# One block of a token mixer: z, i and g projected token by token, head norms from summed squares, and five small steps of two heads on VectorE instead of GpSimd

## The chip, the cores and the metric

The kernel runs on one core of a Trainium2 chip. The metric is the time of one execution on the device, in microseconds (us). Five engines work side by side, each through its own instructions in a fixed order: TensorE (PE) multiplies matrices and transposes, VectorE (DVE) and ScalarE (ACT) do elementwise work, GpSimd (POOL) does small steps and issues some DMAs, SyncE (SP) issues the loads of the weights.

## The reference, cut to what matters

The input x has T = 256 tokens of D = 2048 numbers, all float32. One layer is computed:

```
n = rms_norm(x)
q,k,v,z,a,b | q',f,i,g = n @ W_in          # 8 heads of 128 in each group
# 8 GDN heads: q,k,v = silu(conv4(q,k,v)); q,k normalized to length 1;
#   chunked gated delta rule in chunks of 64 (needs the inverse of unit lower matrices)
#   o = head_rms_norm(o) * silu(z)
# 8 HGRN2 heads: forget = lb + (1-lb) sigmoid(f); key = (1-lb) sigmoid(-f)
#   o = recurrence(silu(q'), key, i, log forget), in chunks of 64
#   o = head_rms_norm(o) * silu(g)
h = x + concat(o) @ W_out
h = h + relu(rms_norm(h) @ W1)^2 @ W2
out = rms_norm(h)
```

The columns of n @ W_in for one head are 4 times 128: q, k, v, z for a GDN head, q', f, i, g for an HGRN2 head.

## The kernel before, in words

**Products in float32.** A weight tile of 1 MB (128 x 2048) is loaded by SyncE. `split` (L120, L121) makes two halves of each 1024 columns: hi, a rounded copy made on ScalarE, and lo, the rest, made on VectorE by a subtraction. A product is hi x hi + hi x lo + lo x hi. There are three buffers for tiles and three for pairs of halves, so a tile's successor is loaded and split as its matmuls end.

**The input projection** (`project`, L286 to L328) makes two groups of 128 features at a time, from two tiles. The activations xT stand with features on partitions; the weights are the stationary operand, and 512 columns of xT (its hi and lo halves, 256 tokens each) move: L314 (hi weights, 512 columns), then L315 (lo weights, 256 columns). A group is the sum of both halves of its PSUM bank: ScalarE copies the one half, VectorE adds the other (L324), and a product with the row scales rB follows (L328). Results have features on partitions and tokens along the row. Each head calls it twice; 16 heads make 64 tiles and 1024 such pairs.

**The GDN heads.** `gdn_project` calls `project` for q, k and for v, z. `gdn_mix` convolves, applies silu to all four groups, transposes v on PE, normalizes q and k and forms the small matrices of the delta rule (products pk, L402 and L403). GpSimd writes blocks of these to a scratch tile in DRAM (scr_a, L412). After head 7, `gdn_invert` (L445 to L470) reads them back (L449) and inverts 16 x 16 blocks on GpSimd by 15 pairs of steps (L459, L461). `gdn_solve` then joins the blocks (L477 to L524: products pQ, pP, pX on PE with steps on VectorE between them) and makes the outputs of two heads at a time.

**The HGRN2 heads.** `hgrn_project` projects q', f and i, g. `hgrn_mix` (from L573) transposes i (L577), computes the gates (L579 to L591), the logarithm and its running sum (L599 to L603), decays at several levels (L608 to L627), small products pd and pa (L638 to L653), joins them into A (L656 to L670) and makes the output poh (L672, L673). Five kinds of small steps in it run on GpSimd: L600, L603, L612, the memset L617, and the pair L663.

**The norm of a head** (`finish_heads`, L420 to L440). The output has features on partitions, so the mean of its squares is taken across partitions, by products with a matrix of ones (L432, L433) on the squares' hi and lo halves; logarithm and exponential give the scale, two products on VectorE apply it and the gate (L436, L437; the gate silu(z) or silu(g) waits in the ring SZ), and a split writes hi and lo into yT, the operand of the output projection. It is called for two GDN heads at once and for one HGRN2 head.

**The order.** The code walks over 16 heads: the projection of head n + 1 stands ahead of the mix of head n, the solver ahead of the mix of head 9 (HGRN2 head 1), the inversion behind the mix of head 7. The framework's scheduler then sets the order on each engine from a simulated timeline, under the dependences and the buffers; at run time each engine takes its instructions strictly in that order.

**PSUM.** It has eight banks of 512 columns. The mixers use two called mx and two called sv (psM); the input projection uses four called acc (psA, opened at the start). When the mixers are done, psB opens on the four banks of psM (L679). **The output projection** (L768 to L791; its matmul is L782, y as the stationary operand and 512 columns of weights moving) makes its first 1024 columns in psA and the others in psB; then the MLP (from L811) begins.

## Time and profile before

| | |
|---|---|
| median of 3 runs | 1231.27 us (1229.66 to 1232.65) |
| the profiled execution | 1230.59 us |
| its span, first to last instruction | 1228.9 us |
| its mean granted clock of TensorE | 0.993 |

| stage, us of the span | length | PE busy | DVE busy | ACT busy | POOL busy | granted clock |
|---|---|---|---|---|---|---|
| 0 to 260: GDN heads | 260 | 257.8 | 228.3 | 180.0 | 87.7 | 1.00 |
| 260 to 310: inversion ends, solver | 50 | 45.5 | 39.6 | 30.4 | 22.1 | 0.93 |
| 310 to 438: HGRN2 heads | 128 | 128.0 | 110.1 | 90.1 | 18.5 | 1.00 |
| 438 to 486: last two heads, output projection | 48 | 47.5 | 38.3 | 29.6 | 6.8 | 1.00 |
| 486 to 537: rest of the output projection | 51 | 49.4 | 35.8 | 28.1 | 0.0 | 0.97 |
| 537 to the end: MLP and last norm | 691.9 | 683.7 | 602.7 | 418.9 | 1.1 | 1.00 |

The second table is put together from windows of the trace. An engine's busy time counts its instructions that compute; the issue of a DMA, semaphores and branches are not counted. The granted clock is the share of full speed that the chip let TensorE run at in the window. A row of a timeline shows the start, the duration from the first instruction to the end of the last, the engine, the line, and the operation with what it writes and reads; "x4" behind it means four in a row.

### The profile page before, as it was taken

The numbers are of one execution on the slowest core, as the hardware profiler recorded it, in microseconds if no ns is written. First come the engines' busy times: TensorE is split into PE (matmuls) and PEld (weight loads), VectorE is DVE, ScalarE is ACT, GpSimd is POOL, SyncE is SP. The second block draws the span as 40 slices with busy tenths as digits, with TensorE's granted clock in tenths as the row PEclk, the third lists the DMA queues.
The fourth block names the chain that finished last, engine by engine and source line by source line (L and its number), as shares of the span: only waits on it lengthen the run. The fifth ranks groups of instructions, "written<-read, shape, count | busy, mean of one in ns | idle before, by whom it ended". The sixth has DMA issues, their size and how long they took to land.

```text
span 1228.9 us, 18515 instructions
## 1 busy us (share of the span) xinstructions
PE 1211.9 (99%) x7058; PEld 1018.8 (83%) x7058; DVE 1054.7 (86%) x1487; ACT 777.1 (63%) x1096; POOL 136.2 (11%) x185
## 2 busy tenths in 40 slices
PE   9999999998999999999999999999999999999997
PEld 7888888887888887888888888888888888888886
DVE  7889998878789986779889889889998888989877
ACT  7667677665677765655565656566666665656653
POOL 0243433262011121000000000000000000000000
PEclk9999999998999999999999999999999999999999
DMA  9545555543336445556455545653866556556461
GB/s 337 171 149 178 182 179 188 183 161 121 127 111 233 170 169 176 211 200 234 146 203 205 210 144 195 240 199 134 324 233 214 197 177 226 186 199 215 170 232 69
DMA packets 37145, 233.46 MB, mean 190 GB/s; under 512 B 4696, under 2 KB 5728, under 8 KB 10176
## 3 DMA queue, kind: packets, MB, share of 16 engines
q1 hardware_dynamic: 34848, 229.83, 53.0%
q0 software_dynamic: 1632, 1.72, 0.9%
q8 instruction: 55, 0.90, 0.3%
q10 hardware_dynamic: 576, 0.74, 0.2%
q14 instruction: 34, 0.28, 0.1%
HBM read 227.67 MB, written 4.60 MB: 189 GB/s over the span
## 4 chain that ended last, share of the span: by engine, by line
PE 93%; POOL 2%; DVE 2%; DMA 1%; issue 1%; ACT 0%; POOLq 0%; SPq 0%; DVEq 0%
PE acc L314 17%; PE acc L812 9%; PE acc L811 9%; PE acc L813 9%; PE acc L315 9%; PE accb L811 9%; PE accb L812 9%; PE accb L813 9%; PE accb L782 4%; PE acc L782 4%; POOL X L461 1%; PE acc L823 1%; PE accb L823 1%; PE pk L402 1%; DMA X<-scr_a 1%
## 5 line engine op out<-in xcount | busy, mean ns | idle before, releaser
L121 DVE TENSOR_TENSOR lo<-w,hi 128x1024 fp32r<-128x1024 f32 (+1 forms) x422 | 487.6, 1171 | 91.5 <-ACT hi L120 81.7
L120 ACT CAST hi<-w 128x1024 fp32r<-128x1024 f32 (+1 forms) x422 | 413.2, 993 | 210.1 <-PE acc L812 55.6
L314 PE MATMUL acc<-xT,hi 128*128 128x512 f32 x1024 | 358.7, 397 | 1.1 <-ACT hi L120 1.1
L315 PE MATMUL acc<-xT,lo 128*128 128x256 f32 x1024 | 280.9, 284 | 0.3 <-DVE lo L121 0.2
L314 PEld LDWEIGHTS acc<-xT,hi 128*128 128x128 f32 x1024 | 189.3, 188 | 39.9 <-ACT hi L120 1.7
L315 PEld LDWEIGHTS acc<-xT,lo 128*128 128x128 f32 x1024 | 193.1, 189 | 7.4 <-DVE lo L121 2.1
L120 ACT CAST hi<-TT 128x1024 fp32r<-128x1024 f32 x88 | 92.0, 1052 | 77.5 <-issue 21.7
L121 DVE TENSOR_TENSOR lo<-TT,hi 128x1024 fp32r<-128x1024 f32 x88 | 106.9, 1222 | 30.3 <-ACT hi L120 27.4
L811 PE MATMUL acc<-hi,sets 128*128 128x512 f32 x260 | 101.5, 392 | 0.0
L812 PE MATMUL acc<-hi,sets 128*128 128x512 f32 x260 | 101.3, 390 | 0.0
L813 PE MATMUL acc<-lo,sets 128*128 128x512 f32 x260 | 96.1, 391 | 0.0
L811 PE MATMUL accb<-hi,sets 128*128 128x512 f32 x224 | 88.1, 393 | 0.0
L812 PE MATMUL accb<-hi,sets 128*128 128x512 f32 x224 | 87.4, 390 | 0.0
L951 POOL TENSOR_TENSOR fin<-fin,cst 128x1 f32<-128x1 f32 x2 | 1.1, 564 | 743.9 <-DVE fin L950 743.9
L813 PE MATMUL accb<-lo,sets 128*128 128x512 f32 x224 | 78.8, 392 | 0.0
L812 PE MATMUL acc<-hi,gs 128*128 128x512 f32 (+1 forms) x200 | 77.1, 385 | 0.0
L811 PE MATMUL acc<-hi,gs 128*128 128x512 f32 (+1 forms) x200 | 76.8, 386 | 0.0
L813 PE MATMUL acc<-lo,gs 128*128 128x512 f32 (+1 forms) x200 | 75.7, 386 | 0.0
L812 PE MATMUL accb<-hi,gs 128*128 128x512 f32 x188 | 73.2, 390 | 0.0
L811 PE MATMUL accb<-hi,gs 128*128 128x512 f32 x188 | 72.8, 390 | 0.0
L813 PE MATMUL accb<-lo,gs 128*128 128x512 f32 x188 | 72.6, 390 | 0.0
L851 DVE TENSOR_TENSOR TT<-w 128x1024 f32<-128x1024 f32 x44 | 53.7, 1220 | 5.9 <-DMA w<-in_w_ff_dram 5.9
(336 smaller groups left out, 2029.9 us busy)
## 6 DMA issues: line engine op xcount, KB each, us to landing
w<-in_w_ff_dram SPq DMA_DIRECT2D x128, 1024.0 KB, 5.0
w<-in_w_in_dram SPq DMA_DIRECT2D x61, 1024.0 KB, 4.9
w<-in_w_out_dram SPq DMA_DIRECT2D x16, 1024.0 KB, 4.9
w<-in_w_in_dram SPq DMA_DIRECT2D x12, 256.0 KB, 5.4
big<-in_xt_dram SPq DMA_DIRECT2D x8, 256.0 KB, 5.5
h<-in_x_dram SPq DMA_DIRECT2D x2, 1024.0 KB, 5.9
scr_h<-h SPq DMA_DIRECT2D x4, 512.0 KB, 5.1
tail<-scr_h SPq DMA_DIRECT2D x2, 1024.0 KB, 6.4
```

What stands on the lines that cost most here:

```text
L120: ACT.copy(hi, w)
L121: eng.tensor_tensor(out=lo, in0=w, in1=hi.bitcast(F32), op=ALU.subtract)
L314: PE.matmul(accs[g], lhsT=hi[:, kk, g, :], rhs=xT[:, k, :], start=(k == 0), stop=False)
L315: PE.matmul(accs[g][:, T:], lhsT=lo[:, kk, g, :], rhs=xT[:, k, 0:T], start=False, stop=(k == KT - 1))
L402: PE.matmul(pk0, lhsT=R[:, 1, 0:P], rhs=qk.rearrange("p a t -> p (a t)"), start=True, stop=True)
L461: POOL.tensor_tensor(out=X[:, j + 1:, 0:ncol], in0=X[:, j + 1:, 0:ncol], in1=t3, op=ALU.subtract)
L782: PE.matmul(accs[2 * hf + c], lhsT=st, rhs=ww[:, c * 512:(c + 1) * 512], start=(k == 0 and a == 0 and ww is hi), stop=(k == 2 * NH - 1 and ...
L811: PE.matmul(dst, lhsT=ah, rhs=bh, start=start, stop=False)
L812: PE.matmul(dst, lhsT=al, rhs=bh, start=False, stop=False)
L813: PE.matmul(dst, lhsT=ah, rhs=bl, start=False, stop=stop)
L823: PE.transpose(pt[:, c * P:(c + 1) * P], src[:, c * P:(c + 1) * P], ident)
L851: DVE.tensor_tensor(out=TT[:, 0:1024].rearrange("p (a c) -> p a c", a=2), in0=view(w, 0, [[1536, 2], [1, 512]]), in1=view(w, 512, [[-512, ...
```

## The change

**Token by token.** z of the GDN heads, and i and g of the HGRN2 heads, are no longer made with features on partitions. `project_tokens` takes the activations as the stationary operand and moves 512 columns of weights: six matmuls for each 128 rows of the weights (L358), into two banks called tok that hold 128 tokens each by 512 columns. One tile of weights is a quarter of such a product. The 512 columns are z of four heads, or i and g of two heads, so results come out for four GDN heads or two HGRN2 heads at once, behind the last of their four tiles; each row is scaled while it is copied out (rcol, one number for each token, made in `row_scales`), and `silu` is applied to 512 columns at a time. q, k, v, q' and f stay as they were, v alone in a bank sv.

**The norm of a head.** The output is made with tokens on partitions (three products of 128 columns, L729 to L731 in `hgrn_mix`). Its squares are summed along the row by ScalarE's accumulated output; a scratch tile takes the squares themselves. One step on VectorE multiplies with scale and gate; PE transposes the result (L487); ScalarE and VectorE write hi and lo halves with the norm's weight. The products with ones and the transposes of i go.

**The five steps** of HGRN2 heads 0 and 1 run on VectorE, those of heads 2 to 7 on GpSimd as before (`eng`).

**PSUM.** The pool psA is opened behind the close of the mixers' pools; the input projection has a pool psP of its own, two banks acc and two banks tok, which closes with the mixers. On the host, the columns of W_in are put into tiles in the new order.

```
-    psA = ctx.enter_context(tc.tile_pool(name="psA", bufs=4, space=PSUM))
...
+    psP = mctx.enter_context(tc.tile_pool(name="psP", bufs=2, space=PSUM))
...
+    def acc_p(tag):
+        return psP.tile([P, 512], F32, tag=tag, name="acc")
...
+    def project_tokens(c):
+        if c == 0:
+            tok[0] = [acc_p("tok") for _ in range(2)]
+        accs = tok[0]
+        w, n = w_next()
+        for q, hi, lo in halves_of(w, n):
+            for kk in range(2):
+                k = c * 4 + q * 2 + kk
+                cs = slice(kk * 512, (kk + 1) * 512)
+                for hf in range(2):
+                    for a, ww in ((0, hi), (T, hi), (0, lo)):
+                        PE.matmul(accs[hf], lhsT=xT[:, k, a + hf * P:a + hf * P + P], rhs=ww[:, cs],
+                                  start=(k == 0 and a == 0 and ww is hi), stop=(k == KT - 1 and ww is lo))
...
+    def tokens_out(dst):
+        for hf in range(2):
+            ACT.activation(dst[:, hf, :], tok[0][hf], AF.Copy, scale=rcol[:, hf:hf + 1])
...
     def gdn_project(hd):
-        project(0, hd, 0, (pre[:, 0, 3:], pre[:, 1, 3:]))
-        project(0, hd, 1, (pre[:, 2, 3:], R[:, 3, :]))
+        project((pre[:, 0, 3:], pre[:, 1, 3:]), POOL, lambda: acc_p("acc"))
+        project((pre[:, 2, 3:],), POOL, lambda: sv("accv"))
+        project_tokens(hd % 4)
+        if hd % 4 == 3:
+            tokens_out(SZ[:, hd // 4])
+            for hf in range(2):
+                silu(SZ[:, hd // 4, hf])
...
     def finish_heads(h0, nh, po, sz, group, scale, bank):
-        ACT.activation(sq, po, AF.Square)
-        ACT.copy(shi, sq)
-        DVE.tensor_tensor(out=slo, in0=sq, in1=shi.bitcast(F32), op=ALU.subtract)
-        PE.matmul(pm, lhsT=ones_r, rhs=shi, start=True, stop=False)
-        PE.matmul(pm, lhsT=ones_r, rhs=slo, start=False, stop=True)
-        ACT.activation(sq, pm, AF.Ln, bias=eps, scale=scale / P)
-        ACT.activation(sq, sq, AF.Exp, scale=-0.5)
-        DVE.tensor_tensor(out=sq, in0=po, in1=sq, op=ALU.mult)
-        DVE.tensor_tensor(out=sq, in0=sq, in1=sz, op=ALU.mult)
+        at = [(hf, n, slice(n * P, (n + 1) * P)) for hf in range(2) for n in range(nh)]
+        for hf, n, c in at:
+            ACT.activation(sq, po[:, hf, c], AF.Square, accum_out=ss[:, hf, n:n + 1])
+        ACT.activation(ss, ss, AF.Ln, bias=eps, scale=scale / P)
+        ACT.activation(ss, ss, AF.Exp, scale=-0.5)
+        for hf, n, c in at:
+            DVE.scalar_tensor_tensor(out=sz[:, hf, c], in0=po[:, hf, c], scalar=ss[:, hf, n:n + 1],
+                                     in1=sz[:, hf, c], op0=ALU.mult, op1=ALU.mult)
+        for hf, n, c in at:
+            PE.transpose(pt[:, n * T + hf * P:n * T + hf * P + P], sz[:, hf, c], ident)
-        split(yv, None, hi, lo)
+        ACT.activation(hi, pt, AF.Copy, scale=gnw[:, group:group + 1])
+        DVE.scalar_tensor_tensor(out=lo, in0=pt, scalar=gnw[:, group:group + 1], in1=hi.bitcast(F32),
+                                 op0=ALU.mult, op1=ALU.subtract)
...
     def hgrn_mix(hd, R):
+        eng = DVE if hd < 2 else POOL
-        POOL.tensor_tensor(out=lf[:, 0, :], in0=lf[:, 0, :], in1=lf[:, 1, :], op=ALU.add)
+        eng.tensor_tensor(out=lf[:, 0, :], in0=lf[:, 0, :], in1=lf[:, 1, :], op=ALU.add)
...
     mctx.close()
...
+    psA = ctx.enter_context(tc.tile_pool(name="psA", bufs=4, space=PSUM))
     psB = ctx.enter_context(tc.tile_pool(name="psB", bufs=4, space=PSUM))
```

**Where instructions move: the inversion and the solver.** On GpSimd before, from the last write of GDN head 7's blocks (PA is the tile of its small matrices) to the first pair of the inversion (X and Xt its blocks; u, gx and E are tiles of HGRN2 head 0):

```order
L412 DMA scr_a<-PA_164 32x2x32 x4
L600 TENSOR_TENSOR u<-u 128x256
L603 TENSOR_SCALAR gx<-gx 128x256
L449 DMA X<-scr_a 64x16x16 x2
L612 TENSOR_TENSOR E<-gx 128x256
L453 AFFINE_SELECT X<-X 128x256
L455 MEMSET X 128x16
L459 TENSOR_TENSOR Xt<-X 128x15
L461 TENSOR_TENSOR X<-X,Xt 128x15
```

The same place after the change:

```order
L463 DMA scr_a<-PA_164 32x2x32 x4
L501 DMA X<-scr_a 64x16x16 x2
L505 AFFINE_SELECT X<-X 128x256
L507 MEMSET X 128x16
L511 TENSOR_TENSOR Xt<-X 128x15
L513 TENSOR_TENSOR X<-X,Xt 128x15
```

The three steps of head 0 (L600, L603, L612) have left GpSimd's queue; the load of the blocks now follows the writes directly.

On PE before, from the solver's second product (L490) to its third (L513), with the small products of an HGRN2 head between them (pd on E and gx):

```order
L490 MATMUL pQ<-Pm,Yd 32x16 x64
L638 MATMUL pd<-E 32x32 x32
L641 MATMUL pd<-gx 32x64
L513 MATMUL pP<-Xn,big 32x32 x20
L513 MATMUL pP<-Xn,PA_164 32x32 x12
```

After the change, the last rows ahead of the third product, now L565 (L358 is the token product; L331 and L332 are the feature pairs of the next head):

```order
L358 MATMUL acc<-hi,xT 128x512 x2
L358 MATMUL acc<-lo,xT 128x512
L358 MATMUL acc<-hi,xT 128x512 x2
L358 MATMUL acc<-lo,xT 128x512
L331 MATMUL acc<-xT,hi 128x512
L332 MATMUL acc<-xT,lo 128x256
L331 MATMUL acc<-xT,hi 128x512
L332 MATMUL acc<-xT,lo 128x256
L331 MATMUL acc<-xT,hi 128x512
L332 MATMUL acc<-xT,lo 128x256
L565 MATMUL pP<-Xn,big 32x32 x20
L565 MATMUL pP<-Xn,PA_164 32x32 x12
```

The two solver products stand further apart: between them lie 13 matmuls of L358, 6 of L331 and L332 and the three of an HGRN2 head's output, where 33 small products of a head lay before.

**Where instructions move: the last heads.** On PE before, at the small products of HGRN2 head 7 (pd, pa), with the output projection around them:

```order
L782 MATMUL acc<-hi,yTa 128x512 x8
L782 MATMUL acc<-lo,yTa 128x512
L638 MATMUL pd<-E 32x32 x32
L641 MATMUL pd<-gx 32x64 x8
L647 MATMUL pa<-E 32x32 x4
L651 MATMUL pa<-E 64x64 x2
L653 MATMUL pa<-L 128x128
L782 MATMUL acc<-lo,yTa 128x512 x3
L782 MATMUL acc<-hi,yTb 128x512 x4
```

After the change, from the last transposes of head 6 to the first matmuls of the output projection, now L847:

```order
L487 MATMUL pt<-cst,ig 128x128 x2
L695 MATMUL pd<-E 32x32 x32
L698 MATMUL pd<-gx 32x64 x8
L704 MATMUL pa<-E 32x32 x4
L708 MATMUL pa<-E 64x64 x2
L710 MATMUL pa<-L 128x128
L729 MATMUL poh<-ig,A 128x128
L730 MATMUL poh<-ig,A 128x128
L731 MATMUL poh<-ig,A 128x128
L487 MATMUL pt<-cst,ig 128x128 x2
L847 MATMUL acc<-hi,yTa 128x512 x4
L847 MATMUL acc<-lo,yTa 128x512 x2
```

All of head 7, to its transposes (L487), stands ahead of the first output-projection matmul; before, these matmuls stood around and between its products.

On VectorE before, at the same place, from head 7's level products (E) to the sum of its rows (rd), with head 6's norm (fsq) and the splits of weights (L121) between them:

```order
L623 TENSOR_TENSOR E<-E,gx 128x256 x5
L624 TENSOR_TENSOR E<-E,gx 128x512
L121 TENSOR_TENSOR lo<-w,hi 128x1024
L436 TENSOR_TENSOR fsq<-poh,fsq 128x256
L627 TENSOR_TENSOR L<-E,ec 128x256
L121 TENSOR_TENSOR lo<-w,hi 128x1024
L437 TENSOR_TENSOR fsq<-fsq,SZ 128x256
L121 TENSOR_TENSOR lo<-w,hi 128x1024
L121 TENSOR_TENSOR yTb<-fsq,yTb 128x256
L656 TENSOR_TENSOR pd<-pd,cst_a 128x384
L660 TENSOR_REDUCE rd<-pd 128x64
```

After the change:

```order
L665 TENSOR_TENSOR E<-gx 128x256 x5
L483 SCALAR_TENSOR_TENSOR ig<-poh,ss,ig 128x128 x2
L682 TENSOR_TENSOR gx<-gx,u 128x256
L680 TENSOR_TENSOR E<-E,gx 128x256 x5
L681 TENSOR_TENSOR E<-E,gx 128x512
L492 SCALAR_TENSOR_TENSOR yTb<-pt,gnw,yTb 128x256
L684 TENSOR_TENSOR L<-E,ec 128x256
L713 TENSOR_TENSOR pd<-pd,cst_a 128x384
L717 TENSOR_REDUCE rd<-pd 128x64
L483 SCALAR_TENSOR_TENSOR ig<-poh,ss,ig 128x128 x2
L492 SCALAR_TENSOR_TENSOR yTb<-pt,gnw,yTb 128x256
L121 TENSOR_TENSOR lo<-w,hi 128x1024 x13
```

The splits of weights no longer stand between the steps of head 7; they come in a row behind its last step (L492).

More of the change, by code (lines that the diff above doesn't have):

```diff
@@ new lines, in w_next @@
+    def w_next():
+        n = tiles[0]
+        tiles[0] += 1
+        if n < 2:
+            return w_first[n], n
+        w = wtile()
+        if n == 2:
+            for c in range(4):
+                SP.dma_start(w[:, c * 512:(c + 1) * 512], w_in[n][:, c * 512:(c + 1) * 512])
+        else:
+            SP.dma_start(w, w_in[n])
+        if n == 3:
+            SP.dma_start(cst, consts[:, 0:NKEEP])
+            SP.dma_start(cst_a, consts[:, NKEEP:])
+            SP.dma_start(wab, w_ab)
+        return w, n
@@ L316, in project @@
                                   start=False, stop=(k == KT - 1))
-        if second:
-            row_scales()
-            for lot, dst in held_back:
-                POOL.tensor_tensor(out=dst, in0=lot, in1=rB, op=ALU.mult)
-        for g in range(2):
+        for g in range(ng):
             lot = mp.tile([P, T], F32, tag="lot", name="lot", bufs=2)
             ACT.copy(lot, accs[g][:, T:])
-            DVE.tensor_tensor(out=lot, in0=accs[g][:, 0:T], in1=lot, op=ALU.add)
-            if first:
-                held_back.append((lot, dsts[g]))
-            else:
-                (POOL if base == 0 else DVE).tensor_tensor(out=dsts[g], in0=lot, in1=rB, op=ALU.mult)
@@ new lines, in gdn_solve @@
+            finish_heads(2 * pair, 2, po, SZ[:, pair // 2, :, pair % 2 * T:pair % 2 * T + T], 0, 1.0 / P, sv)
+    ig = [None]
+    def hgrn_project(hd):
+        R = mp.tile([P, 3, T], F32, tag="R", name="R", bufs=RB)
+        project((R[:, 0, :], R[:, 1, :]), DVE, lambda: acc_p("acc"))
+        for c in range(2):
+            project_tokens(hd % 2 * 2 + c)
+        if hd % 2 == 1:
+            ig[0] = mp.tile([P, 2, 512], F32, tag="ig", name="ig", bufs=2)
+            tokens_out(ig[0])
+            silu(ig[0][:, :, T:])
@@ L571, in hgrn_project @@
         return R
     def hgrn_mix(hd, R):
-        pv = mx("pvh")
-        for hf in range(2):
-            PE.transpose(pv[:, hf * P:(hf + 1) * P], R[:, 3, hf * P:(hf + 1) * P], ident)
-        vv = mp.tile([P, 2, P], F32, tag="vv", name="vv")
-        ACT.copy(vv.rearrange("p a e -> p (a e)"), pv[:, 0:T])
-        u = mp.tile([P, 4, T], F32, tag="u", name="u", bufs=UB)
-        sigmoid_parts(u[:, 0:3, :], R[:, 0:3, :], 3 * T)
-        DVE.scalar_tensor_tensor(out=u[:, 3, :], in0=R[:, 1, :], scalar=0.0, in1=u[:, 1, :], op0=ALU.max, op1=ALU.add)
@@ L691, in hybrid_block, with acc_a @@
     mctx.close()
+    psA = ctx.enter_context(tc.tile_pool(name="psA", bufs=4, space=PSUM))
     psB = ctx.enter_context(tc.tile_pool(name="psB", bufs=4, space=PSUM))
+    def acc_a():
+        return psA.tile([P, 512], F32, tag="acc", name="acc")
     def acc_b():
```

187 lines of the change are left out of this document (106 added, 81 removed).

## The prediction

> **What bounds the kernel now.** I read the busy line of the page first, then the waits of TensorE (PE), then the windows of the stages in which PE loses time. Times are those of the one profiled execution: a span of 1228.9 us, 1230.59 us with what lies around it, against a median of 1231.27 us of the runs shown; the sum below is made against 1230.6.
>
> ```profile
> PE 1211.9 (99%) x7058; PEld 1018.8 (83%) x7058; DVE 1054.7 (86%) x1487; ACT 777.1 (63%) x1096; POOL 136.2 (11%) x185
> PE accb L782 <- DVE fsq L436: 2.0, 1, 2.0
> PE pd L638 <- issue: 1.9, 1, 1.9
> PE poh L672 <- POOL Xt L459: 1.1, 1, 1.1
> PE pP L513 <- DVE Xn L492: 0.9, 1, 0.9
> PE pQ L484 <- DVE Xn L477: 0.2, 1, 0.2
> PE acc L315 <- DVE lo L121: 0.2, 1, 0.2
> 294.60:301.30 6.70, 5.61 (x106) 4.92 (x106) 6.55 (x15) 3.84 (x7) 0.10 (x1) 0.50 0.48 159
> 489.10:492.40 3.30, 3.30 (x9) 2.58 (x8) 2.37 (x3) 2.83 (x3) 0.00 (x0) 0.50 0.66 278
> ```
>
> PE is the bound: it is busy for all but 17 us. A change is therefore worth what it takes out of PE's own stream, or what it adds or closes in PE's idle time. From 260 us to 310 us, where GpSimd (POOL) inverts blocks and the solver starts, PE waits 1.9 + 1.1 + 0.9 + 0.2 + 0.2 = 4.3 us; at 485 us, where the mixers end, 2.0 us. The two windows (us, then busy time of PE, weight loads, VectorE, ScalarE and GpSimd, then the granted clock) show what follows each: 6.7 us and 3.3 us at a clock of 0.50, which lose half of their length, 3.35 us and 1.65 us. So the solver's place loses 4.3 + 3.35 = 7.7 us, and the end of the mixers 2.0 + 1.65 = 3.7 us.
>
> **PE's own work.**
>
> ```profile
> 134.12 0.40 PE L314 MATMUL acc<-xT,hi 128*128 128x512 f32 x1
> 134.35 0.28 PE L315 MATMUL acc<-xT,lo 128*128 128x256 f32 x1
> 134.47 0.39 PE L314 MATMUL acc<-xT,hi 128*128 128x512 f32 x1
> 448.82 8.42 PE acc L782 x37
> 469.83 0.38 PE L577 MATMUL pvh<-cst,R 128*128 128x128 f32 x2
> 469.96 0.71 PE L782 MATMUL acc<-lo,yTa 128*128 128x512 f32 x2
> 463.21 0.28 PE L432 MATMUL pm<-shi,ones_r 128*128 128x256 f32 x1
> 463.33 0.40 PE L782 MATMUL acc<-hi,yTa 128*128 128x512 f32 x1
> 457.08 0.59 PE L672 MATMUL poh<-A,vv 128*128 128x256 f32 x2
> 457.65 0.95 PE L782 MATMUL acc<-hi,yTa 128*128 128x512 f32 x3
> ```
>
> Matmuls overlap, so I count from start to start. A projection pair (512 columns, then 256) takes 134.47 - 134.12 = 0.35 us. The new token product has the form of the output projection, weights moving in 512 columns, and 37 of those took 8.42 us, 0.2276 us each. Three eighths of the 1024 pairs move: 384 x 0.35 = 134.4 us become 576 x 0.2276 = 131.1 us, **-3.3 us**; were they to run at the 0.23 us of the pair's long half, it would be 132.5 us and -1.9. The two transposes of a head's values cost 0.13 us and go 8 times, -1.0. The two ones-products of the normalization cost 0.12 us each at one head and, by the long half of the pair, 0.23 us at two: 8 x 0.24 + 4 x 0.46 = -3.8. Thirty-two transposes come in their place at 0.065, +2.1. The three products of 128 columns that give a head's output take the place of two that took 0.57 us together; with the same number of columns I put them at no change. Sum **-6.0 us** (bounds -4 and -7).
>
> **The five GpSimd steps, and the solver.**
>
> ```profile
> 240.35 2.13 POOL L412 DMA_DIRECT2D scr_a<-PA  x4 [17.08 <-DVE PA L406]
> 248.35 1.71 POOL L449 DMA_DIRECT2D X<-scr_a  x2
> 267.94 0.76 POOL L663 TENSOR_TENSOR A<-rd,cst_a 128x128 f32<-128x128 f32 x2
> 284.50 0.97 DVE L477 TENSOR_SCALAR Xn<-Xq,cst_a 128x256 f32<-128x256 f32 x2
> ```
>
> Before, the load of the blocks is issued at 248.35 because two steps of head 0 stand ahead of it on GpSimd's queue; the writes that it needs were issued by 242.5. A DMA of this tile lands in 3 us or so, so it could leave near 245.5. That and the pair of 0.76 us inside the inversion shorten the way from 240.35 to 284.50 (44.2 us) by about 3.7 us. But PE also arrives sooner: between the last GDN head's k products and the solver's first product the old order has 235 projection matmuls (117.5 pairs, 41.1 us), the new one 64 pairs and 66 long ones (22.4 + 15.0 = 37.4 us). The two shifts cancel, so the solver's first wait stays small; I allow 1 us. The waits for A at 268 us and on VectorE behind the first solver steps lose their cause: A no longer stands behind the inversion, and the solver's steps lie further apart in PE's new order. VectorE takes over 5 steps a head of some 0.3 to 0.4 us, under 4 us in all; it is idle beside PE for far more than that. I take **-6.7 us** of the 7.7; bounds 0 (the waits come back at other steps, and the clock falls again) and -9 (the bubbles between steps go too).
>
> **The end of the mixers.**
>
> ```profile
> 438.40:485.40 47.00, 42.87 (x180) 33.17 (x180) 1.00 0.53 180
> 446.92 0.73 PE L638 MATMUL pd<-E 128*32 128x32 f32 x62
> 448.57 1.18 PE L782 MATMUL acc<-hi,yTa 128*128 128x512 f32 x4
> 457.55 0.62 ACT L599 ACTIVATE u<-u 128x512 f32<-128x512 f32 x1
> 458.25 1.25 POOL L600 TENSOR_TENSOR u<-u 128x256 f32<-128x256 f32 x1 [5.08 <-ACT u L599]
> 459.71 0.68 DVE L602 TENSOR_TENSOR_SCAN gx<-cst_a,u 128x256 f32<-128x256 f32 x1
> 465.02 1.21 DVE L121 TENSOR_TENSOR lo<-w,hi 128x1024 fp32r<-128x1024 f32 x1
> 466.15 1.76 DVE L623 TENSOR_TENSOR E<-E,gx 128x256 f32<-128x256 f32 x5
> 467.83 0.69 DVE L624 TENSOR_TENSOR E<-E,gx 128x512 f32<-128x512 f32 x1
> 473.74 1.05 ACT L120 CAST hi<-w 128x1024 fp32r<-128x1024 f32 x1 [0.98 <-ACT yTb L120]
> 474.85 0.57 DVE L656 TENSOR_TENSOR pd<-pd,cst_a 128x384 f32<-128x384 f32 x1 [0.79 <-PE pd L641]
> 475.45 0.56 DVE L660 TENSOR_REDUCE rd<-pd 128x64 f32<-128x384 f32 x1
> 478.18 0.41 ACT L670 COPY A<-pa 32x64 f32<-32x64 f32 x2
> 482.79 0.39 ACT L426 ACTIVATE fsq<-poh 128x256 f32<-128x256 f32 x1 [0.28 <-PE poh L673]
> 1215.27 0.18 ACT L938 ACTIVATION_READ_ACCUMULATOR sqf<-tail 128x1 f32 x1
> 488.44 0.43 DVE L121 TENSOR_TENSOR yTb<-fsq,yTb 128x256 fp32r<-128x256 f32 x1 [0.47 <-ACT yTb L120]
> ```
>
> The first row is the window in which heads 6 and 7 of HGRN2 are mixed, counting L782 alone: 180 output-projection matmuls (41 us of stream) fill PE. They could, because their four banks (psA) stood beside the mixers' four. In the changed kernel psA is opened after the mixers' pools are closed, and PE's order has not one output-projection matmul until the last head's transposes. PE runs in order, so after the last input-projection matmul (call it P) it has nothing but the rest of two heads, and waits through a chain.
>
> I add that chain up by the new order. **(a)** Head 7's steps stand behind 1.05 us of cast and 1.21 of split for the next weights (their buffer comes free at P), a copy of new token sums (512 columns on ScalarE, 0.62), head 6's 0.57 and 0.56, and four steps of 256 columns at 0.3 to 0.4 (1.4); then its Ln, 0.62: 6.0 us. **(b)** GpSimd's add, 1.25. **(c)** From the scan to the end of L624, 459.71 to 468.52, is 8.8 us, less the split that lies between (465.02 to 466.15, 1.1): 7.7; head 6's two gating products stand inside it, an estimate of 0.6 from 0.43 for 256 columns. **(d)** Two more steps at 0.4: 0.8. **(e)** From L656 to the end of L670, 474.85 to 478.59, is 3.7 us with a pair of GpSimd products at 1.83; that pair took 0.76 at 267.94, when VectorE was idle, as it will be here: 2.7. **(f)** The output products at half clock 1.1, two squares with their accumulator reads (0.39 and 0.18 at most each) 1.0, two tiny steps 0.4, two gating products 0.6, two transposes 0.5, the two halves of the result 0.4 and 0.43: 4.4. Together 6.0 + 1.25 + 8.3 + 0.8 + 2.7 + 4.4 = **23.5 us** from P to the first output-projection matmul.
>
> Of these PE works 4.3 us on what it had to do anyway (a head's small products took 448.57 - 446.92 = 1.65 us, the output products 0.57 and the transposes 0.13; two heads, less what is done before P). The other 19.2 us are idle. The clock will be at half when the projection starts: by the two windows above, 1.65 to 3.35 us lost, I take 2.5. The 3.7 us lost there before go. **19.2 + 2.5 - 3.7 = +18.0 us**; bounds +13 (the chain is 5 us shorter) and +22 (every step of (a) and (b) waits for the one before it, and a product of GpSimd costs 1.8).
>
> The Trainium skill, "TensorE: Matmul & The Clock Gate", Part 1 (the HAM clock gate), says that the clock halves after about 3.4 us of idleness and comes back after about 3.4 us of work; by that the restart would cost half of 3.4, 1.7 us, and the sum would be 0.8 us less. The trace agrees with the way back at 489 us (3.3 us at 0.50) but not at 294 us (6.7 us), and there a wait of 2.0 us was enough to bring the clock down.
>
> The MLP is unchanged and begins when the output projection has ended, so all of this moves the end. **Sum: -6.0 - 6.7 + 18.0 = +5.3 us; 1230.6 + 5.3 = 1235.9, and I forecast 1236 us.**
>
> **Rivals.**
> - **The last head runs ahead (faster).** ScalarE and VectorE lose more work than they get: 24 additions of two halves (0.4 us), 16 gates and the wide normalization go. If head 7's Ln is done at P instead of P + 6, and (c) and (e) run without gaps, the projection starts near P + 14, 9.5 us sooner: 1226.5 us. It decides from P + 18 on downward (even) and P + 15.5 (faster by over 0.2%). Against it: in the new order head 7's sigmoid stands on ScalarE behind a cast that waits for the next-to-last weight tile's matmuls, so it can't start before about P - 5, however idle the engines are.
> - **The solver's wait comes back.** VectorE has the two heads' extra steps in just the stretch in which it bound (its windows there are full), PE waits again behind the solver, and the clock falls: the 6.7 us are not gained, 1242.6 us. For it: the two waits on VectorE at 292 to 297 us. Against it: the wider spacing in PE's new order.
> - **Even.** The exposed chain is 4 to 6 us shorter and the rest as computed: 1230 to 1233 us.
>
> **How the numbers follow.** Forecast 0.50 (its own range 1233.8 to 1240), solver's wait back 0.18 (to 1245 with a longer chain), even 0.19, last head ahead 0.13. A measurement of this kernel can tell about 0.2% (2.5 us) from no change, so slower 0.68, within 0.19, faster 0.13. The range leaves out 0.1 on each side: 1228 to 1244.
>
> **What would show it.** Right: in the changed profile PE has one idle stretch of some 19 us shortly after the last token product, with rows at clock 0.50 behind it; no output-projection matmul lies before the last transposes; the waits on GpSimd's inversion are gone; the last token product ends some 12 us earlier than the old 438 us. Wrong: PE's idle time at the end of the mixers is under 14 us, or the solver's stretch still shows a window at 0.50, or a token product takes over 0.235 us from start to start.

## The result, and the profile after

The changed kernel takes 1252.51 us (median of 4 runs, 1252.03 to 1253.72) against 1231.59 us: 1.0173 times as long, with a 95% interval of 1.0155 to 1.0191. That is 20.9 us more; 4.4 more had been forecast (1236), with a range that ended at 1244. The profiled execution has a span of 1250.2 us, 21.3 us over that of before.

The busy line of the page and the largest waits of TensorE (PE) in the two stages that the prediction named (us in total, times, longest):

```profile
PE 1221.6 (98%) x6894; PEld 1017.3 (81%) x6894; DVE 1035.3 (83%) x1455; ACT 777.0 (62%) x1150; POOL 113.4 (9%) x165
PE pt L487 <- DVE ig L483: 5.0, 2, 3.0
PE poh L729 <- POOL u L657: 4.4, 1, 4.4
PE pQ L536 <- DVE Xn L529: 2.4, 1, 2.4
PE pd L695 <- DVE E L680: 1.4, 1, 1.4
PE pp L584 <- ACT XP L578: 1.4, 1, 1.4
PE poh L729 <- POOL A L720: 1.2, 1, 1.2
PE acc L847 <- DVE yTb L492: 1.1, 1, 1.1
PE pP L565 <- DVE Xn L544: 0.7, 1, 0.7
```

PE has 164 matmuls fewer and is busy 9.7 us longer. Longer busy time with less work means time at a lower clock, so the windows are read next (us, then busy time of PE, weight loads, VectorE, ScalarE and GpSimd, then the granted clock; the last two numbers are what the DMA engines did):

```profile
294.70:302.00 7.30, 4.92 (x148) 4.21 (x148) 5.15 (x12) 2.20 (x4) 0.00 (x0) 0.77 0.07 18
321.80:324.00 2.20, 0.32 (x13) 0.08 (x2) 2.20 (x3) 2.15 (x4) 0.00 (x0) 0.63 0.23 30
324.00:339.60 15.60, 15.60 (x115) 13.44 (x116) 10.06 (x21) 4.27 (x13) 3.32 (x5) 0.50 0.17 65
444.40:467.20 22.80, 9.57 (x175) 7.41 (x160) 13.29 (x31) 11.32 (x33) 4.89 (x7) 0.59 0.13 48
467.20:472.40 5.20, 5.20 (x12) 4.13 (x13) 0.00 (x0) 0.54 (x1) 0.00 (x0) 0.50 0.00 0
```

The last two rows are the end of the mixers: 13.2 us without work, and nearly all of the 14.8 us of work in them at half clock. The third row is the surprise. In the solver's stage TensorE works without a break for 15.6 us, and all of it at a clock of 0.50.

To compare stages I use one measure, the **loss**: from windows of one microsecond each, PE's idle time, plus the part of its busy time that the clock withheld. Before, the solver's stage (180 to 360 us) lost 7.3 us and the end of the mixers 3.8 us. After, they lost 14.9 and 20.0 us. In the solver's stage most of this is the clock: idle time went from 4.5 to 5.4 us, what the clock withheld from 2.8 to 9.5. At the very start 0.4 us less is lost. So 21.3 = 7.6 (solver) + 16.2 (end) - 0.4 + the rest, and the rest, PE's own work, is -2.1 us. The MLP (from the start of its first matmul to that of its last) takes 682.9 us in both.

### The profile page after: what moved, and what is told of

Its sections match the earlier page's. It is cut to its first block, busy times and chain, and to the rows that moved or that the text cites. A ratio compares the mean times of both kernels' runs of the same rounds, so it can differ in the third digit from the quotient of the medians.

```text
span 1250.2 us, 18173 instructions
## 1 busy us (share of the span) xinstructions
PE 1221.6 (98%) x6894; PEld 1017.3 (81%) x6894; DVE 1035.3 (83%) x1455; ACT 777.0 (62%) x1150; POOL 113.4 (9%) x165
## 4 chain that ended last, share of the span: by engine, by line
PE 91%; POOL 2%; DVE 2%; DMA 2%; issue 1%; ACT 1%; SPq 0%; POOLq 0%; DVEq 0%; ACTq 0%
PE acc L877 9%; PE acc L878 9%; PE acc L876 9%; PE acc L358 9%; PE accb L877 8%; PE accb L876 8%; PE accb L878 8%; PE acc L331 8%; PE acc L332 4%; PE acc L847 4%; PE accb L847 3%; PE accv L331 2%; PE accv L332 1%; POOL X L513 1%; POOL Xt L511 1%
## 5 line engine op out<-in xcount | busy, mean ns | idle before, releaser
L121 DVE TENSOR_TENSOR lo<-w,hi 128x1024 fp32r<-128x1024 f32 (+1 forms) x422 | 485.7, 1167 | 123.4 <-ACT hi L120 112.3
L331 PE MATMUL acc<-xT,hi 128*128 128x512 f32 x512 | 181.2, 400 | 0.7 <-ACT hi L120 0.7
L332 PE MATMUL acc<-xT,lo 128*128 128x256 f32 x512 | 140.9, 287 | 0.0
L120 ACT CAST hi<-TT 128x1024 fp32r<-128x1024 f32 x88 | 92.0, 1052 | 77.5 <-issue 21.7
L121 DVE TENSOR_TENSOR lo<-TT,hi 128x1024 fp32r<-128x1024 f32 x88 | 106.8, 1221 | 30.4 <-ACT hi L120 28.1
L358 PE MATMUL acc<-hi,xT 128*128 128x512 f32 x384 | 117.6, 395 | 0.0
L331 PEld LDWEIGHTS acc<-xT,hi 128*128 128x128 f32 x512 | 95.4, 190 | 20.7 <-ACT hi L120 1.2
L332 PEld LDWEIGHTS acc<-xT,lo 128*128 128x128 f32 x512 | 97.2, 191 | 5.2 <-DVE lo L121 1.9
L358 PEld LDWEIGHTS acc<-hi,xT 128*128 128x128 f32 x384 | 71.5, 189 | 14.9
L358 PE MATMUL acc<-lo,xT 128*128 128x512 f32 x192 | 73.5, 401 | 0.0
```

The source lines that it names most:

```text
L120: ACT.copy(hi, w)
L121: eng.tensor_tensor(out=lo, in0=w, in1=hi.bitcast(F32), op=ALU.subtract)
L331: PE.matmul(accs[g], lhsT=hi[:, kk, g, :], rhs=xT[:, k, :], start=(k == 0), stop=False)
L332: PE.matmul(accs[g][:, T:], lhsT=lo[:, kk, g, :], rhs=xT[:, k, 0:T], start=False, stop=(k == KT - 1))
L358: PE.matmul(accs[hf], lhsT=xT[:, k, a + hf * P:a + hf * P + P], rhs=ww[:, cs], start=(k == 0 and a == 0 and ww is hi), stop=(k == KT - 1 a ...
```

## The experiments

Times are medians; the kernel before had medians of 1230.7 to 1231.1 us beside them. In the notes, "stage" is the solver's stage, 180 to 360 us.

**The five steps.** Three runs change only which engine takes them.

```
         eng = DVE if hd < 2 else POOL      # the change
-> e1:   eng = POOL
-> e2:   eng = DVE
-> e3:   the kernel before, with eng = DVE if hd < 2 else POOL in hgrn_mix
```

> The changed kernel with the five small steps on GpSimd for all eight HGRN2 heads, so that part of the change is undone. Its solver's stage lost about 15 us (waits and half clock) where 1 us was forecast. Theory A: the five steps of two heads are not what crowds VectorE (they are under 4 us in all); without them the load for the inversion stands behind GpSimd steps again, the solver's first product is reached 2 to 4 us later, and the time is 1253 to 1257 us. Rival B: the extra steps on VectorE are what holds the solver up; then the loss falls back to the 8 us of before and the time is 1244 to 1247 us.

Measured: 1248.78 us (1248.01 to 1253.59), 3.7 us under the changed kernel. Neither range is hit. The profiled execution is one of the longer ones (span 1251.9 us), so its stage, which lost 17.8 us, doesn't stand for the median. The steps on VectorE cost up to 3.7 us, about half of the 7.6 us by which the stage's loss grew; two of the five executions (1253.5 and 1253.6 us) gain nothing, so even this is not firm.

> The changed kernel with the five small steps on VectorE for all eight HGRN2 heads. In the changed kernel's trace VectorE stands still 1.6 and 0.8 us at 306 to 309 us, because steps of HGRN2 head 2 wait for GpSimd (L657, L660), and the solver's L544 stands behind them, its product done since 306.4 and the step begun only at 311.7; at the end of the mixers TensorE waits 4.4 and 1.2 us for GpSimd steps. Theory A (a queue behind GpSimd): 4 to 5 us go from the end and 3 to 8 us from the solver's stage: 1240 to 1246 us. Rival B (VectorE is simply full): the end gains 4 us, the solver's stage loses as much or more: 1249 to 1256 us.

Measured: 1248.12 us (1246.52 to 1252.09), 4.4 us under the changed kernel, between both theories. Its stage lost 10.4 us, the end of the mixers 18.4: most of the gain is in the stage. Both ways of making the eight heads alike give about as much.

> The kernel before with this one part of the change: the five small steps of HGRN2 heads 0 and 1 on VectorE. Theory A: the inversion starts up to 3.7 us sooner and the waits on GpSimd at 268 us (1.3 us) and on VectorE at 285 us (0.5 us) go; 1227 to 1230 us against 1231. Rival B: VectorE, full from 285 to 300 us, gets later by the added steps and the solver's waits and half clock grow: 1233 to 1238 us.

Measured: 1233.34 us, 1.0019 times before (1.001 to 1.0027), rival B's side. Done alone, this part of the change costs 2.3 us; the forecast had counted on it for a gain. The stage lost 9.0 us where before lost 7.3.

**The banks.** The four banks of the input projection stay open and serve the output projection:

```
-    psP = mctx.enter_context(tc.tile_pool(name="psP", bufs=2, space=PSUM))
+    psP = ctx.enter_context(tc.tile_pool(name="psP", bufs=2, space=PSUM))   # ahead of the mixers' pools
...
-    psA = ctx.enter_context(tc.tile_pool(name="psA", bufs=4, space=PSUM))
...
+    def acc_a():
+        turns[0] += 1
+        return acc_p("acc" if turns[0] % 4 in (1, 2) else "tok")
```

> The changed kernel with the four banks of the input projection kept open and used by the first half of the output projection, so that its matmuls can be put between the steps of the last two heads; up to the last token product the order on TensorE is the same. From the last token product to the first output-projection matmul the changed kernel takes 23.0 us, of which TensorE is idle or at half clock for about 17. Theory A: this end costs 15 to 17 us by the missing banks alone, and the time is 1235 to 1238 us. Rival B: the last head's chain ends as late as before and something behind it (the second half of the output projection, which needs the last heads, or the weights' buffers) takes up the wait: 1243 to 1249 us.

Measured: 1233.54 us (11 runs), 19.0 us faster than the changed kernel and 1.002 times before (1.0012 to 1.0029). The end of the mixers in this run:

```profile
444.60:465.00 20.40, 20.40 (x163) 17.10 (x163) 17.25 (x31) 14.59 (x28) 4.45 (x5) 1.00 0.49 161
465.00:485.00 20.00, 20.00 (x178) 16.31 (x177) 9.66 (x12) 8.55 (x17) 0.76 (x2) 1.00 0.51 178
323.90:341.30 17.40, 17.40 (x124) 15.14 (x125) 11.22 (x22) 6.50 (x14) 3.32 (x5) 0.51 0.16 59
```

PE is busy without a break and at full clock where it had lost 20.0 us; the loss there is 0. The other stage, whose order on PE is that of the changed kernel, is as it was: 17 us at half clock again (third row), 15.8 us lost. Theory A is right and was set 2 us too low. The reverse, the same part alone in the kernel before:

```
-    psA = ctx.enter_context(tc.tile_pool(name="psA", bufs=4, space=PSUM))
...
+    psP = mctx.enter_context(tc.tile_pool(name="psP", bufs=4, space=PSUM))   # for project
...
     mctx.close()
+    psA = ctx.enter_context(tc.tile_pool(name="psA", bufs=4, space=PSUM))
```

> The kernel before with this one part of the change: the input projection's four banks close with the mixers, and the output projection's banks open behind them, so that no output-projection matmul can stand between the steps of the last two heads. The order on TensorE is that of before up to the last input-projection matmul. Theory A (the missing banks make the end's loss by themselves): TensorE has some 13 us idle there and comes back at half clock, 14 to 19 us more than before: 1245 to 1250 us. Rival B (the new norm of a head, with its transposes and accumulated squares, makes the chain long, and the old one would be done sooner): 4 to 10 us more, 1235 to 1241 us.

Measured: 1255.19 us, 1.02 times before (1.0186 to 1.0214), 24.1 us more; above theory A's range. The end of the mixers, window and largest waits:

```profile
439.20:470.70 31.50, 12.62 (x206) 8.98 (x204) 21.67 (x54) 15.39 (x34) 4.04 (x8) 0.56 0.10 35
PE pd L638 <- DVE E L623: 10.9, 2, 5.7
PE poh L672 <- issue: 2.6, 1, 2.6
PE pm L432 <- ACT shi L430: 1.8, 2, 0.9
```

With the old heads 31.5 us pass between the last input-projection matmul and the first of the output projection; with the new ones it is 22.8. So the late banks cost at least as much without the rest of the change, and in these two orders the change, taken whole, leaves the shorter exposed chain. Rival B had it the wrong way round.

**Cover between the solver's steps.** The order tells how many projection matmuls stand between two of them (s1 and s2 are the two rounds of 64 x 64 blocks, L532 and L537 before, L584 and L589 after):

| kernel | pQ to second pQ | to pP | to pX | to s1 | to s2 | to the next product |
|---|---|---|---|---|---|---|
| before | 22 | 0 | 16 | 21 | 19 | 22 |
| changed | 19 | 19 | 25 | 0 (4 more inside s1) | 6 | 7 |
| solver one head later | 31 | 0 | 16 | 19 | 21 | 17 |

```
-SOLVE_AT, INVERT_AT = 9, 7
+SOLVE_AT, INVERT_AT = 10, 7      # with the early banks
```

> The run with the early banks (1233.5 us), with the solver put ahead of the mix of head 10 instead of head 9. Between the solver's product pX, its two rounds of 64 x 64 blocks and the next product the order of before has 21, 19 and 22 projection matmuls, that of the changed kernel 0 to 4, 6 and 7; with the solver one head later it is 19, 21 and 17 again. Idle time of TensorE and time lost at half clock between 180 and 360 us: 7.3 us before, 14.9 in the changed kernel, 15.8 with the early banks. Theory A (missing cover in the order): this falls to 3 to 8 us and the time to 1221 to 1227 us. Rival B (VectorE and ScalarE are too full in this stage, wherever the steps stand): the loss stays over 11 us and the time over 1229 us.

Measured: 1226.19 us (11 runs), 7.4 us faster than the run with early banks and **0.9971 times before (0.9962 to 0.9981)**: the fastest of all, and faster than both kernels. The two largest places where the stage still loses, and the end of the mixers:

```profile
298.60:304.00 5.40, 2.97 (x8) 2.39 (x8) 5.40 (x12) 2.30 (x4) 0.00 (x0) 0.69 0.00 0
319.30:327.20 7.90, 4.98 (x89) 4.37 (x86) 7.21 (x18) 2.81 (x6) 0.67 (x2) 0.62 0.32 122
439.90:480.00 40.10, 40.10 (x348) 33.30 (x348) 28.22 (x45) 24.61 (x48) 5.08 (x7) 1.00 0.50 168
```

The time is as theory A had it, the loss (10.7 us, from 15.8) is not: the stretch of 17 us at half clock is gone, but waits remain: the first window is a wait of 2.4 us for VectorE's split of the next weights, the second stands at the step to pP, which has no cover here.

> The kernel before with the solver ahead of the mix of head 10, as a control. Here the cover between the solver's steps is the same at both places (19 to 22 projection matmuls), so if cover is what counts, the time stays within 4 us of before: 1227 to 1233 us, the gain coming only from the wait for the inversion. Rival: a later solver is better by itself, whatever the order; then 1222 to 1226 us.

Measured: 1232.58 us, 1.0019 times before (1.001 to 1.0028); the stage lost 7.5 us. The later place isn't better by itself. It helped where the order had left the solver's last steps bare.

**What holds the clock down.** In the changed kernel, PE around the fall of the clock (start, us, line, operation):

```profile
320.64 0.59 PE L487 MATMUL pt<-cst,ig 128*128 128x128 f32 x2
321.16 0.73 PE L695 MATMUL pd<-E 128*32 128x32 f32 x61
322.32 0.19 PE L695 MATMUL pd<-E 128*32 128x32 f32 x1 [0.44 <-issue]
323.95 1.94 PE L584 MATMUL pp<-XP,big 64*64 64x64 f32 x16 [1.44 <-ACT XP L578]
```

```profile
322.00:323.00 1.00, 0.19 (x1) 0.00 (x0) 1.00 (x2) 1.00 (x2) 0.00 (x0) 0.69 0.00 0
```

There are a wait of 0.44 us and one of 1.44 us, with small products on both sides, and 16 of s1 take 1.94 us, 121 ns each where 58 would be full speed. (A float32 product of this kind stands in the trace as two records; counts here are of records.) A mean clock of 0.69 in the window from 322 to 323 us puts the fall at 322.4 us, ahead of the longer wait: by the trace's records PE had been busy for 3.0 of the last 3.4 us, on 32 x 32 products, two transposes and pd, without one projection matmul. So idle time alone doesn't explain this fall. Three runs ask which products count.

```
-            for n in range(8):                                       # s1
+            for n in [n for _ in range(6) for n in range(8)]:
```

> The kernel before with the solver's first round of 64 x 64 block products issued six times, each writing the same result again: about 154 of them stand in a row, 8.9 us by the 58 ns of one. TensorE has work all that time. Theory A (the granted clock follows how much of the array works, and small products count as rest): the clock falls to 0.50 some 3 to 5 us after the row begins, with TensorE busy, and comes back only 3 to 4 us after full products have begun again; 1245 to 1252 us. Rival B (only idle time brings the clock down): it stays at 1.00 through the row; 1238 to 1242 us.

Measured: 1241.0 us, as rival B had it. The row of small products:

```profile
312.30:324.20 11.90, 11.90 (x209) 11.85 (x208) 5.39 (x12) 1.04 (x2) 0.10 (x1) 1.00 0.01 2
```

Theory A falls: 11.9 us of 64 x 64 products leave a full clock at 1.00 (one execution).

> The control to the run with small products: the kernel before with the solver's product pw (128 x 128, the whole array) issued eight times, two rows of some 6.5 us. Both theories expect the clock to stay at 1.00 through the rows; a fall would mean that neither size of the product nor idle time sets it. 1239 to 1244 us.

Measured: 1245.31 us; both rows of 64 records of whole products (7.31 us each) run at 1.00, the first of them here:

```profile
323.90:331.20 7.30, 7.30 (x67) 7.30 (x66) 1.23 (x1) 0.12 (x1) 0.00 (x0) 1.00 0.43 146
```

> The run with early banks, with the solver's first round of 64 x 64 products issued six times. In that run the clock is at 0.50 from 324 to 341 us with TensorE always busy, part of it on these products; at full clock a row of 12 us of them did not bring the clock down. Theory A (such products don't count enough to bring a halved clock back up, only full ones do): the clock stays at 0.50 through the whole row, 15 us or more, and comes back 3 to 5 us after the full products that follow it. Rival B (any work without a break brings it back): the clock is at 1.00 within 7 us of the row's begin.

Measured: 1251.49 us. The window, from before the row of small products to the return of the clock, and pieces of it:

```profile
323.50:357.20 33.70, 33.33 (x282) 31.74 (x283) 10.15 (x21) 5.16 (x14) 3.08 (x5) 0.50 0.10 33
323.87 10.89 PE L585 MATMUL pp<-XP,big 64*64 64x64 f32 x100 [1.06 <-ACT XP L579]
345.84 2.08 PE L598 MATMUL pw<-V,Y 128*128 128x128 f32 x8
351.07 2.08 PE L603 MATMUL pr<-V,big 128*128 128x128 f32 x8
353.93 0.56 PE L333 MATMUL acc<-xT,lo 128*128 128x256 f32 x1
357.45 0.39 PE L332 MATMUL acc<-xT,hi 128*128 128x512 f32 x1
```

Theory A holds here: PE works 33 us without a break at 0.50. Two stretches of 2 us of whole products inside don't bring the clock back; 3.5 us of projection products in a row (353.9 to 357.4) do. So the 64 x 64 products keep a clock as it is: in these two runs, of one execution each, they don't lower a full one, and they don't raise a halved one. For 32 x 32 products the fall at 322.4 us speaks against the first half. That is the size of the stage's loss: the fall before, after which the projection is back at 300 us, withholds 2.8 us of work; here, where blocks and short pieces of projection follow for 15 us, it withholds 8.

**VectorE's stand.** In the changed kernel VectorE waits for the inverted blocks with the solver's first step at the head of its queue:

```profile
296.85 0.61 DVE L529 TENSOR_SCALAR Xn<-Xq,cst_a 128x256 f32<-128x256 f32 x2 [5.66 <-DMA Xq<-scr_x]
```

With early banks and the later solver this stands as well (5.5 us). The next runs hold the step back by a dependence:

```
+        half = cpool.tile([P, 2], F32, tag="half", name="half")       # [P, 16] in e13 and e15
+        DVE.scalar_tensor_tensor(out=half, in0=R[:, 1, 0:2], scalar=0.0, in1=C("half")[:, 0:2],
+                                 op0=ALU.mult, op1=ALU.add)
...
-            DVE.tensor_scalar(Xn[:, :, n * HB:(n + 1) * HB], Xq, C("half")[:, n:n + 1], None, ALU.mult)
+            DVE.tensor_scalar(Xn[:, :, n * HB:(n + 1) * HB], Xq, half[:, n:n + 1], None, ALU.mult)
```

> The run with early banks and the solver one head later (1226.2 us), with one step more: the solver's first step on VectorE takes its constant from a copy that also reads the next HGRN2 head's projected features, so that it can't be put early in VectorE's order (15 rows later there; TensorE's order nearly the same). In that run VectorE stands still for 5.5 us at 291 to 297 us, at the head of its queue the solver's first step, which waits for the inverted blocks; behind it VectorE is full until 324 us and TensorE waits at 298, 310 and 320 us (idle and half clock in this stage: 10.7 us). Theory A (VectorE's queue stands behind the inversion and the backlog makes the later waits): the 5.5 us are used, the stage's loss falls to 3 to 6 us and the time to 1219 to 1223 us. Rival B (the waits come from the length of the solver's own chain): the loss stays at 9 to 12 us and the time at 1225 to 1228 us.

Measured: 1240.6 us, 14.4 us slower, and for a reason that neither theory had. VectorE's stand is gone and the stage lost 9.2 us, 1.5 less than without the hold; but the MLP, whose code nobody touched, took 696.1 us in place of 682.9. Its matmuls start 231 ns apart in place of 227.

> The same with the five small steps of all eight HGRN2 heads on VectorE. Theory A: the short waits of VectorE for GpSimd (0.6, 0.8 and 1.0 us at heads 2 and 3) go, and the chain of a head gets shorter by the slower steps of GpSimd; 1 to 3 us faster than the run before it. Rival B: VectorE, with no time left in this stage, pays for every step it takes over: 0 to 3 us slower.

Measured: 1238.74 us, 1.9 us under its neighbour; the MLP is as slow.

> The run with the solver's first step held, once more, with the constant's tile 64 bytes long in place of 8. In that run the stage's loss fell only from 10.7 to 9.2 us, the 5.5 us stand of VectorE was gone, but every matmul of the MLP took 231 to 233 ns from start to start in place of 227, 13 us in all: the small tile had moved all later buffers of SBUF by 32 bytes. Theory A (the move by 32 bytes made the matmuls slower): with a move by 64 bytes they take 227 ns again and the time is 1222 to 1226 us. Rival B (the extra step or any move does it): 1236 to 1241 us.

Measured: 1237.71 us. Theory A falls in the form that I gave it: a move by 64 bytes slows the MLP as well (692.9 us, 10 more than before). The stage lost 11.5 us with no stand of VectorE, PE's waits now being these:

```profile
PE pP L568 <- issue: 4.3, 1, 4.3
PE pt L488 <- DVE ig L484: 1.8, 1, 1.8
```

The loss of 10.7 us is 9.2 in one held run and 11.5 in the other: VectorE's stand at the head of its queue is not, by itself, what it hangs on. The waits move to the step to pP, the one with no cover. (In the held runs with all steps on VectorE the stage lost 7.3 us, above, and 8.3 us, below.)

> The kernel before with one unused tile of 8 bytes a partition among the constants, which moves the later buffers by 32 bytes, and one memset that fills it. TensorE's order is that of before. Theory A (the place of the buffers): MLP matmuls take 231 to 233 ns from start to start and the MLP 13 us more; the projections may lose as much a matmul: 1243 to 1253 us. Rival B: as before, 1229 to 1233 us.

```
     gnw = cpool.tile([P, 2], F32, tag="gnw", name="gnw")
+    spare = cpool.tile([P, 2], F32, tag="spare", name="spare")
+    POOL.memset(spare, 0.0)
```

Measured: 1243.93 us, 1.0104 times before (1.009 to 1.0118), 12.8 us for 8 unused bytes. In a window of the MLP (the number behind PE's busy time counts its matmuls), before and then this run:

```profile
600.00:700.00 100.00, 100.00 (x459) 83.01 (x458) 87.42 (x97) 60.59 (x73) 0.00 (x0) 1.00 0.57 206
```

```profile
600.00:700.00 100.00, 100.00 (x450) 81.33 (x449) 85.40 (x94) 59.46 (x72) 0.00 (x0) 1.00 0.57 204
```

450 matmuls in 100 us and not 459, at the same clock and load. The projections are as fast as before (232 and 117 ns), so only the MLP feels it.

> The held solver with the 64-byte tile and the five small steps of all eight HGRN2 heads on VectorE. Against the same with the steps of six heads on GpSimd, the two runs with the 8-byte tile differed by 1.9 us. Theory A: 1.5 to 2.5 us faster than its neighbour, 1220 to 1224 us. Rival B: no difference beyond 1 us, the 1.9 us having come with the slower matmuls.

Measured: 1236.41 us, 1.3 us under its neighbour, between both theories. Less what the MLP took more (13.2, 12.7, 10.0 and 9.8 us), the four held runs stand at 1226.0 to 1227.7 us: holding the step gains nothing over 1226.19.

> Early banks, the solver one head later and not held, and the five small steps of all eight HGRN2 heads on VectorE. Theory A (VectorE's waits for GpSimd are short links of the chains that TensorE waits for): 1.5 to 4 us faster than with the steps of six heads on GpSimd (1226.2 us): 1222 to 1225 us. Rival B (in the stage where VectorE works off 5.5 us of standing still, each step more makes TensorE wait): 1226 to 1229 us.

Measured: 1230.01 us, over a wide range (1225.54 to 1233.79), 0.9991 times before (0.9978 to 1.0004). No gain over the 1226.19 us with the steps of six heads on GpSimd; rival B, and a little beyond it.

## Why the prediction was wrong, point by point

The forecast was a sum of three terms, -6.0 - 6.7 + 18.0 = +5.3 us; the profile has -2.1 + 7.6 + 16.2 (and -0.4 at the start). Of the 16.0 us between the two, 14.3 are the solver's place, 3.9 PE's own work, -1.8 the end of the mixers.

**What bounds the kernel: right.** PE is the bound; what the change adds is idle time of PE and time at half clock.

**The solver's place: wrong, and this is the step that failed.** "I take -6.7 us of the 7.7; bounds 0 (the waits come back at other steps, and the clock falls again) and -9", it said; measured +7.6. Its reason was that "the solver's steps lie further apart in PE's new order". That was read off the order at the first steps, up to pP, where it is true (19 matmuls where there were none). It isn't true of the last three steps, which have 0, 6 and 7 where there were 21, 19 and 22, and which the prediction didn't look at. There 1.9 us of waits stand and, what costs more, the clock falls where no row of projection matmuls follows. The bound at 0 was wrong as well, since it took the clock's fall at its old price, 3.35 us withheld in 6.7 us. (That is 2.8 by the windows: PE was idle for 1.1 of the 6.7 us, and 4.3 + 3.35 counts this part twice; the stage lost 7.3, not 7.7.) The fall now costs 8 us, since what follows it are blocks, which don't bring the clock back (shown for 64 x 64 products by their row at half clock). Putting the solver one head later, with cover of 19, 21 and 17 again, took out the long stretch at half clock and 7.4 us of the time, 5.1 of them in the loss of the stage; the same move in the kernel before, which had its cover, gained nothing. The move changes more of the order than the cover of three steps, so cover fits best, and no run changed it alone.

The solver's first wait was mis-sized too. The two shifts that were to cancel, 3.7 us each, were 2.5 and 4.6: the way from the write of the blocks to VectorE's first step takes 41.7 us (255.18 to 296.85) in place of 44.2, but PE comes to the product 42.9 us after head 7's k products in place of 47.5. Its wait there is 2.4 us, where 0.2 stood before and 1 was allowed.

The rival "the solver's wait comes back" named the result but put it on VectorE and stopped at the old loss (1242.6 us). Its mechanism finds part support: the five steps alone cost the old kernel 2.3 us in place of a gain, and undoing them gives the changed one 3.7 us. But moving the steps of all heads to VectorE gives it 4.4 us, so it isn't VectorE's load as such. VectorE's stand of 5.7 us behind the inversion, the clearest thing in its timeline, is not the cause as far as was tried: with the solver one head later the stage lost about as much without it, and the time was no better. In the changed kernel itself it wasn't tried. Why GDN head 7's k products come 14 us later than before (252.0 us against 237.6, by the trace) is not settled; PE didn't wait for them, so the order set it.

**The end of the mixers: right in mechanism and in the sum, not in its parts.** From the last token product to the first output-projection matmul the chain of steps gave 23.5 us; it is 23.0 (444.2 to 467.2). The idle time was forecast as 19.2 us, with 2.5 us more for the half clock; by the windows it is 13.2 us idle and 6.7 us withheld, since the clock falls early in the stretch and PE's work in it, taken at 4.3 us, fills 9.6 at half speed. The sum is 19.9 where 21.7 stood: one term 6.0 too large, the other 4.2 too small, so that the sum came out closer than its parts is in part luck. Its cause, the banks, is shown twice: opened early they give 19.0 us back, opened late in the old kernel they cost 24.1. The half clock at the start of the output projection lasts 5.2 us and costs 2.6, as forecast; what the forecast left out is the half clock ahead of it.

The Trainium skill, "TensorE: Matmul & The Clock Gate", Part 1, puts the return at about 3.4 us of sustained work; the 353.9 to 357.4 us stretch agrees, the 33 us of blocks ahead of it show that work of any kind is not enough.

**PE's own work: sign right, size not.** Forecast -6.0, bounds -4 and -7; by what is left over, -2.1. The term that was mis-sized most is the projection. It was to bring -3.3; by the starts of all its matmuls (idle time left out, half clock counted at half) it took 364.42 us before and 363.76 after, -0.7. The token products do start 227 ns apart, as forecast, where they stand in a row. But a long matmul behind a transpose or a small product takes 0.32 us to the next start, and over all 576 the mean is 0.234 us: 135.0 us where 131.1 stood.

```profile
342.02 0.38 PE L729 MATMUL poh<-ig,A 128*128 128x128 f32 x2
342.24 0.39 PE L730 MATMUL poh<-ig,A 128*128 128x128 f32 x2
342.46 0.39 PE L731 MATMUL poh<-ig,A 128*128 128x128 f32 x2
342.61 0.36 PE L332 MATMUL acc<-xT,lo 128*128 128x256 f32 x1
...
377.95 0.38 PE L487 MATMUL pt<-cst,ig 128*128 128x128 f32 x2
378.09 0.71 PE L358 MATMUL acc<-lo,xT 128*128 128x512 f32 x2
378.64 0.62 PE L358 MATMUL acc<-hi,xT 128*128 128x512 f32 x2
```

Two transposes take 0.14 us to the next start, and the two matmuls behind them 0.55 us where two take 0.455: 0.12 us a transpose, 0.05 more than the prediction counted. That holds for the 16 that go as for the 32 that come, so 0.8 us in all, within what the projection missed. The three products of a head's output were rightly put at no change: 0.59 us in the rows above (342.02 to 342.61), where the two of before took 0.57. Of the 3.9 us the projection has 2.6, and 1.3 stay unassigned. That part was found by adding up and not tried alone.

**The named signs.** Idle time at the last heads, half clock behind it, no output-projection matmul before the last transposes: seen, though as several waits of up to 4.4 us and not as one stretch of 19. The wait for GpSimd's inversion at 268 us is gone; the 2.4 us at the solver's first product are a wait for VectorE, whose step waits for the inverted blocks. Two of the three signs of being wrong came: "the solver's stretch still shows a window at 0.50" is there, twice, and PE's idle time at the end of the mixers is 13.2 us, under the 14 that were named. The third, a token product of over 0.235 us, did not (0.227 in a row, 0.234 in the mean). The last token product was to end 12 us earlier than 438 us; it ended 6 us later.

## What to carry to other kernels

When a new order is read ahead of a run, count the bound engine's cover between every two links of a latency chain, not at the links that waited before: what is put right at one link may have been taken from the next. Keep accumulation banks open across a stage boundary: a bank that opens only when the stage before has ended turns that stage's whole last chain into idle time, here 19 to 24 us of 1231. And after every run compare a stage that the edit doesn't touch, since an allocation alone can move it.

## What the runs showed of the hardware that was not expected

- **A halved clock stays halved under small products.** 64 x 64 products left a full clock at 1.00 for 11.9 us, but 33 us of work at 0.50, blocks for the most part and with two pieces of 2 us of whole products in it, didn't raise it. A row of projection matmuls did, after 3.5 us in one run, 5.2 us in another. How much of them is enough is open: before the change 1.5 us of them, behind a head's small products, were enough (299.84 to 301.3 us), and after it 2.2 us among blocks were not (329.97 to 332.2 us).
- **The clock changes in steps of 3.41 us.** In the clock records of all eighteen traces each stretch at 0.50 that ends inside the run is a whole multiple of it, from 3.4 us to ten times as long, 34.1 us. So what a wait costs hangs also on where it falls in this grid: on the same order of PE the clock fell at 322.4 us in the changed kernel, and at 324.3 us in the run with early banks.
- **A small allocation slowed matmuls that don't use it.** With 8 unused bytes a partition among the constants, which move the buffers allocated after them on that side of SBUF (by 32 bytes as the framework rounds; the traces show no addresses), the MLP's matmuls started 231 ns apart and not 227, 12.6 us in all (695.5 us against 682.9). A tile of 64 bytes cost 10 us. The projections, all of whose buffers move together, stayed at 232 and 117 ns; the MLP also uses buffers that are allocated from the other end (`side="right"`) and don't move. That the distance between the two counts is a guess from this and was not tried. The tile came each time with one instruction that writes it; no run has that instruction alone.
